# A two-layer hybrid trunk on one core: fewer and larger visits of attention and recurrence between the projections

## The chip, the core and the metric

The kernel runs on one core of a Trainium2 chip. The metric is the device time of one execution in microseconds (us); less is better. Its engines are TensorE (PE: matmuls and, by a matmul with the identity, transposes), VectorE (DVE), ScalarE (ACT), GpSimd (POOL) and SyncE (SP), which issues the weight loads. PE's operands lie in SBUF, its results in eight PSUM banks of 128 x 512 floats. An engine works through its own list of instructions in order, and semaphores make it wait for the others.

## What is computed

Two layers over 256 rows of width 1024, all in float32. Each layer projects the normed rows with one wide matrix, runs a gated linear recurrence (8 heads of 128) and a sliding-window attention with sinks (16 query heads of 64, 4 key heads), merges both with gates, and ends in a gated FFN of width 2816.

```python
h = rmsnorm(x, norm1[l]); proj = h @ w_in[l]
hq, hf, hi, hg, aq, ak, av, ga, gb = split_cols(proj)
q = silu(hq); f = lb + (1 - lb) * sigmoid(hf); kk = 1 - f; v = hi      # per head of 128
o_hg = hgrn2_chunked(q, kk, v, log(max(f, MIN_F)))                     # gated linear recurrence
y_a = (rmsnorm(o_hg, hg_norm[l]) * silu(hg)) @ w_pa[l]
y_b = swa_with_sinks(rope(aq), rope(ak), av, attn_sinks[l]) @ w_pb[l]  # window 128, exp scores
x = x + (sigmoid(ga) * y_a + sigmoid(gb) * y_b) @ w_o[l]
h2 = rmsnorm(x, norm2[l])
x = x + (silu(h2 @ w_gate[l]) * (h2 @ w_up[l])) @ w_down[l]
# after both layers: rmsnorm(x, final_norm)
```

## The kernel before

**Weights.** Every matrix product is made of split operands: `a = ah + al` and `w = wh + wl`, and PE computes `ah wh + ah wl + al wh`. All weights stand in one list, `plan` (lines 154 to 175), in the order in which they are used. SP loads them as blocks of 1 MB (`raw`, three buffers, so loads run ahead). A block is two *units* of 128 x 1024, numbered through the program. For each unit ACT makes `wh` by a cast (`high`, line 221) and DVE makes `wl` by a subtraction (`low`, line 224); five buffers of each (`NW`) let this run about four units ahead (`used`, `ahead`). A unit is used in one of two ways. Form a (line 250) multiplies the activations as weights-in-PE with 512 columns of w: 12 matmuls of 128 x 512, six for each half `t` of the rows. Form b (line 300) computes the transposed product and takes 8 wide (512 columns) and 8 narrow (256 columns) matmuls.

**Order of the projections.** Before, a layer goes akv (keys and values of attention), aq (queries of attention), v (the recurrence's values, eight units), pb (its `f` and `q`, sixteen units in form b, two groups `g` of four heads), gate, gb and yb, ga, ya, wo, then the FFN (`layer`, line 442).

**Sides.** The projections yield after a few matmuls (one step). Two generators run beside them, `attention` (line 577) and `recurrence` (line 783); after each step of the projections the loop `run` (line 435) lets a side take its turn when the number of steps that it yielded has passed. So `YN`, `YD`, `YE`, `YQ` and `GAPS` (lines 31 to 33) are gaps in steps. What a side then puts on PE between two big matmuls is called a *visit* here. `together` lets several generators put their matmuls into one visit; `pe_order` keeps PE's instructions of a visit in the order in which they are written. Otherwise a scheduler sets each engine's order from these calls.

**Attention.** The 16 query heads go in four *attends* n = 0 to 3 of four heads. For each: `qk`, 16 matmuls with 64 contraction rows; then on DVE eight maxima with the mask (`tensor_tensor_reduce`), on ACT eight exponentials in place and one for the sink, on DVE the scaling; `turn(n)`, twelve transposes `pt` of the weights, copied back by ACT; and `values(n)`, 16 matmuls `pv` with 64 output rows. `qp` are the transposes of the queries. One buffer `sp` holds the scores of two attends, so attend n + 2 comes in the visit in which values n are computed: the visits with narrow tiles are qk, qk, pv+qk, pv+qk and pv(2)+pv(3).

**Decays and recurrence.** `decays(g)` (line 601) makes, on ACT, sigmoids of `f` and of `q`, four steps `f = lb + oml f`, and `k = 1 - f`; on DVE `q k` and a maximum. It is issued behind the last attend's exponentials, since sigmoid needs another table of ACT than exp. `chain(g)` (line 613) is the recurrence of four heads: `lb`, `lc` and three `lv` levels of matmuls with 32 or 64 output rows, `lx`, `o` and `ot`, with DVE and ACT work between them. The two chains run one step apart, so visits hold lb(0), then lb(1)+lc(0), lc(1)+lv(0), and so on.

**Opening.** x arrives as 512-column pieces; `Norm.turning` (line 366) turns four 128-column slices on PE, scales them on DVE and splits them on ACT and DVE. `rest(-1)` places the second half's turn behind the first akv matmul. `spin` fills gaps with matmuls `warm` whose result nobody uses.

Of the kernel before, what the change touches and what calls it, by code (L numbers as in the profile page):

```python
# [15 lines left out]
P = 128  # L16
# [26 lines left out]
def trunk(ctx, tc, x, norm1, w_in, lb_logits, hg_norm, attn_sinks, w_pa, w_pb, w_o, norm2,  # L43
# [111 lines left out]
    for l in range(DEPTH):  # L155
        win = w_in[l]
        for c0 in (C_AK, C_AQ, C_AQ + 512, C_HI, C_HI + 512):
            plan += [(win, 0, 4, c0, 512), (win, 4, 4, c0, 512)]
        for g in range(2):
            for col in (C_HF, C_HQ):  # L160
                plan += [(win, 0, KT, col + 512 * g + 256 * b, 256) for b in range(2)]
        for c in range(2):
# [12 lines left out]
        plan.append((w_down[l], groups[-1][0], 2, 0, D))  # L175
# [74 lines left out]
    def form_a(pss, act, skew=False, ks=range(KT), first=True, last=True, late=None):  # L250
# [10 lines left out]
        if late:  # L261
# [61 lines left out]
    def scaled(ps, gain, name):  # L323
        tmp = ztile([P, 4, P], name, "rp")
        V.tensor_tensor(tmp, ps.rearrange("p (k c) -> p k c", k=4),
                        gain.rearrange("p (k o) -> p k o", o=1).to_broadcast([P, 4, P]), ALU.mult)
        return tmp
# [7 lines left out]
    class Norm:  # L335
# [26 lines left out]
        def turn(self, t, c):  # L362
            for _ in self.turning(t, c):
                pass

        def turning(self, t, c):
            ps = psum(f"xp_{self.name}{t}{c}", self.banks[t])
            for j in range(4):
                k = 4 * c + j
                T.transpose(ps[:, j * P:(j + 1) * P], xs[t][:, k * P:(k + 1) * P], ident)  # L370
            sl = slice(t * P, (t + 1) * P)
            ks = slice(4 * c, 4 * c + 4)
            yield
            tmp = scaled(ps, self.gain[:, ks], f"xg_{self.name}{t}{c}")
# [67 lines left out]
    def layer(l, n1):  # L442
# [37 lines left out]
        att = halves(f"att{l}")  # L480
        oT = halves(f"o{l}")
        mT = halves(f"m{l}", "rh")
        fqk = [[btile([P, 4, S], f"{n}{l}{g}", "h") for n in "fqk"] for g in range(2)]
        state = {}
# [19 lines left out]
        def attend(n):  # L504
            g, i0 = n // 2, 2 * (n % 2)
            s = state["sp"][:, n % 2]
            m = sm.tile([P, 4, 2, 2, 2], F32, tag="stat", name=f"stat{l}{n}", bufs=3)
            pss = [[psum(f"qk{l}{n}{t}{u}", "hg" if t else "at") for u in range(2)] for t in range(NT)]
            for t in range(NT):
                W = (t + 1) * P  # L510
                for i in range(2):
                    for u in range(2):
                        pr = slice(u * 64, u * 64 + 64)
                        T.matmul(pss[t][u][:, i * W:(i + 1) * W], qT[g][pr, i0 + i, t * P:(t + 1) * P], kT[pr, g, 0:W],
                                 start=True, stop=True)
            yield
            for t in range(NT):
                W = (t + 1) * P
                for i in range(2):
                    for u in range(2):  # L520
                        V.tensor_tensor_reduce(s[:, 2 * u + i, t * P:t * P + W], pss[t][u][:, i * W:(i + 1) * W],
                                               amask[:, 256 - W:256], op0=ALU.add, op1=ALU.max, scale=1.0,
                                               scalar=-3.0e38, accum_out=m[:, 0, t, u, i:i + 1])
            nsk = nsink.rearrange("p (l g u h) -> p l g u h", l=DEPTH, g=2, u=2)[:, l, g, :, i0:i0 + 2]
            for t in range(NT):
                V.scalar_tensor_tensor(m[:, 1, t], m[:, 0, t], -0.125, nsk, ALU.mult, ALU.min)
                V.tensor_tensor(m[:, 2, t], m[:, 1, t], nsk, ALU.subtract)
            for t in range(NT):
                for u in range(2):
                    for i in range(2):  # L530
                        sv = s[:, 2 * u + i, t * P:t * P + (t + 1) * P]
                        A.activation(sv, sv, AF.Exp, bias=m[:, 1, t, u, i:i + 1], scale=0.125,
                                     accum_out=m[:, 0, t, u, i:i + 1])
            state["exp"] = A.activation(m[:, 2], m[:, 2], AF.Exp).ins
            V.tensor_tensor(m[:, 3], m[:, 0], m[:, 2], ALU.add)
            V.reciprocal(m[:, 3], m[:, 3])
            for t in range(NT):
                for u in range(2):
                    for i in range(2):
                        sv = s[:, 2 * u + i, t * P:t * P + (t + 1) * P]  # L540
                        V.tensor_scalar(sv, sv, m[:, 3, t, u, i:i + 1], None, ALU.mult)

        def turn(n):
            s = state["sp"][:, n % 2]
            for u in range(2):
                ps = psum(f"pt{l}{n}{u}", "at")
                for i in range(2):
                    for t in range(NT):
                        T.transpose(ps[:, i * S + t * P:i * S + t * P + P], s[:, 2 * u + i, t * P:t * P + P], ident)
                A.copy(s[:, 2 * u:2 * u + 2, 0:S], ps.rearrange("p (i c) -> p i c", i=2))  # L550
            ps = psum(f"pt{l}{n}2", "hg")
            for i in range(4):
                T.transpose(ps[:, i * P:(i + 1) * P], s[:, i, 2 * P:3 * P], ident)
            A.copy(s[:, :, S:3 * P], ps.rearrange("p (i c) -> p i c", i=4))

        def values(n, bank):
            g, pT = n // 2, state["sp"][:, n % 2]
            po = psum(f"pv{l}{n}", bank)
            for u in range(2):
                vs = slice(256 + (2 * g + u) * HD, 256 + (2 * g + u + 1) * HD)  # L560
                for i in range(2):
                    o = po[i * 64:i * 64 + 64, u * S:(u + 1) * S]
                    T.matmul(o, akv[0][:, vs], pT[:, 2 * u + i, 0:S], start=True, stop=False)
                    T.matmul(o[:, P:S], akv[1][:, vs], pT[:, 2 * u + i, S:3 * P], start=False, stop=True)
# [12 lines left out]
        def attention():  # L577
            state["sp"] = sm.tile([P, 2, 4, 384], F32, tag="sp", name=f"sp{l}", bufs=1)
            for t in range(NT):
                rope(aq[t], QH, t)  # L580
            yield YQ
            queries(0)
            yield 2
            for n, gaps in enumerate(YN):
                visit = [values(n - 2, "mm")] if n > 1 else []
                together(*visit, attend(n))
                if n == 3:
                    state["last"] = True
                yield gaps[0]
                if n:  # L590
                    turn(n - 1)
                    yield gaps[1]
                if n == 1:
                    queries(1)
                    yield gaps[2]
            turn(3)
            yield YE
            together(values(2, "at"), values(3, "at"))
            yield 5
# [13 lines left out]
        def chain(g):  # L613
# [121 lines left out]
            for i in range(8):  # L735
                h, a = i // 2, i % 2 * P
                T.matmul(ps[0:64, i, :], k[:, h, a:a + 64], q[:, h, a + 64:a + P], start=True, stop=True)
            px = psum(f"lx{l}{g}", tag).rearrange("p (i c) -> p i c", c=P)
# [44 lines left out]
        def recurrence():  # L783
# [4 lines left out]
            yield YD  # L788
            chains = [chain(g) for g in range(2)]
            next(chains[0])  # L790
            yield 1
            while atd[0] is not None:
                yield 1
            for n, gaps in enumerate(GAPS):
                live = [c for g, c in enumerate(chains) if 0 <= n - g < len(GAPS) - 1]
                pe_order[0] = True
                for c in live[::-1]:
                    next(c)
                pe_order[0] = False
                for c, gap in zip(live, gaps):  # L800
                    next(c, None)
                    if n == 0:
                        next(chains[1])
# [13 lines left out]
        for c in range(2):  # L817
            yield from proj(f"v{c}", lambda t, ps: evac_scaled(v[t][:, c * 512:(c + 1) * 512], ps, rs[t]))
# [10 lines left out]
        rec = start(recurrence(), 1)  # L829

# [229 lines left out]
    some = [nx.turning(t, 0) for t in range(NT)]  # L1060
# [5 lines left out]
    go(0)  # L1066
    spin(4)
    prepare()
    high(0, 0)
    go(0, 0)  # L1070
    high(0, 1)
    go(0)
    pinned[0] = False

    def rest(u):
        pinned[0] = True
        if u < 0:
            go(1)
            spin(3)
            go(1, 1)  # L1080
            low(0, 0)
            go(1)
            low(0, 1)
            high(prepare())
            low(1)
            high(prepare())
        elif u == 0:
            some[:] = [nx.turning(t, 1) for t in range(NT)]
# [75 lines left out]
```

## Time and profile before

| what | value |
| --- | --- |
| median of 3 runs | 933.36 us (932.88 to 933.45) |
| the profiled execution, its own time | 933.17 us |
| span of that execution, first to last instruction | 931.4 us |
| mean granted TensorE clock, share of full speed | 0.998 |
| busy PE, DVE, ACT | 923.1, 675.2, 540.8 us |

The span is what the trace covers; 1.77 us of the profiled time lie outside it. A share of busy time is a mean over stages with different limits. In the timelines below, "start" counts from the span's start, the duration of a matmul includes its way through the array, so the distance from one start to the next tells what PE gave to it.

### The profile page before, as it was taken

How to read it: one execution, taken by the hardware profiler on the slowest of the kernel's cores; microseconds unless marked ns; L12 is line 12 of the kernel's file. 1: busy time of each engine (PE TensorE's matmuls, PEld its weight loads, DVE VectorE, ACT ScalarE, POOL GpSimd, SP SyncE). 2: the span in 40 equal slices, each digit the busy share in tenths (PEclk: the TensorE clock that was granted, in tenths of full speed). 3: DMA queues.
4: the chain of work that ended last, by engine and by line, in shares of the span. 5: the costliest groups of instructions: out<-in, count | busy, mean ns of one | idle time of the engine just before them, and what ended most of it. 6: DMA issues, size and time to landing. Idle time of an engine off the chain costs nothing.

```text
span 931.4 us, 14391 instructions
## 1 busy us (share of the span) xinstructions
PE 923.1 (99%) x5726; PEld 781.5 (84%) x5726; DVE 675.2 (72%) x1171; ACT 540.8 (58%) x914; POOL 20.5 (2%) x31
## 2 busy tenths in 40 slices
PE   9999999999999999999999999999999999999997
PEld 7888888888888888888888888888888888888885
DVE  6667789975778766766865677898667777667665
ACT  6566795465456545545555867945554565555553
POOL 2000000001000000000000000000010000000000
PEclk9999999999999999999999999999999999999999
DMA  8735426644546655566465444545445565556531
GB/s 299 259 127 192 136 92 194 205 145 136 181 136 200 198 190 181 186 197 203 163 200 187 136 137 145 173 162 194 151 153 180 165 197 181 181 189 203 194 138 46
DMA packets 111395, 161.40 MB, mean 173 GB/s; under 512 B 2912, under 2 KB 64672, under 8 KB 111328
## 3 DMA queue, kind: packets, MB, share of 16 engines
q1 hardware_dynamic: 110848, 159.42, 52.5%
q8 instruction: 45, 0.74, 0.3%
q10 hardware_dynamic: 320, 0.79, 0.2%
q0 software_dynamic: 160, 0.26, 0.1%
q14 instruction: 22, 0.18, 0.1%
HBM read 159.42 MB, written 1.05 MB: 172 GB/s over the span
## 4 chain that ended last, share of the span: by engine, by line
PE 99%; DVE 0%; ACT 0%; POOL 0%; issue 0%; DVEq 0%; ACTq 0%; POOLq 0%
PE pg L57 13%; PE pu L57 13%; PE acc L57 13%; PE pb L57 10%; PE gate L57 5%; PE gb L57 5%; PE v L57 5%; PE yb L57 5%; PE wo L57 5%; PE ya L57 5%; PE ga L57 5%; PE aq L57 5%; PE akv L57 2%; PE qk L57 1%; PE pv L57 1%; PE o L57 1%
## 5 line engine op out<-in xcount | busy, mean ns | idle before, releaser
L57 DVE TENSOR_TENSOR wl<-raw,wh 128x1024 fp32r<-128x1024 f32 (+1 forms) x301 | 364.3, 1220 | 126.8 <-ACT wh L57 125.4
L57 ACT CAST wh<-raw 128x1024 fp32r<-128x1024 f32 (+1 forms) x301 | 314.5, 1050 | 168.5 <-PE acc L57 46.0
L57 PE MATMUL pu<-xx_n,wh 128*128 128x512 f32 x352 | 92.6, 393 | 0.0
L57 PE MATMUL pg<-xx_n,wh 128*128 128x512 f32 x352 | 92.1, 393 | 0.0
L57 PEld LDWEIGHTS pg<-xx_n,wh 128*128 128x128 f32 x352 | 63.2, 189 | 11.0
L57 PEld LDWEIGHTS pu<-xx_n,wh 128*128 128x128 f32 x352 | 63.1, 189 | 10.9
L57 PE MATMUL acc<-wh,ah 128*128 128x512 f32 x174 | 68.1, 391 | 0.0
L57 PE MATMUL acc<-wh,al 128*128 128x512 f32 x174 | 67.8, 390 | 0.0
L57 PE MATMUL acc<-wl,ah 128*128 128x512 f32 x174 | 67.8, 389 | 0.0
L57 PE MATMUL pb<-xx_n,wh 128*128 128x512 f32 x256 | 66.3, 396 | 0.0
L57 PEld LDWEIGHTS pb<-xx_n,wh 128*128 128x128 f32 x256 | 45.4, 189 | 8.9 <-DVE wl L57 0.7
L57 PEld LDWEIGHTS pg<-xx_n,wl 128*128 128x128 f32 x352 | 48.4, 190 | 4.1 <-ACT xx_n L57 0.6
L57 PEld LDWEIGHTS pu<-xx_n,wl 128*128 128x128 f32 x352 | 48.4, 191 | 3.6
L57 PE MATMUL pg<-xx_n,wl 128*128 128x256 f32 x352 | 50.3, 284 | 0.0
L57 PE MATMUL pu<-xx_n,wl 128*128 128x256 f32 x352 | 49.8, 283 | 0.0
L57 ACT COPY zg<-pg 128x256 f32<-128x256 f32 x44 | 16.4, 372 | 53.1 <-PE pg L57 53.1
L57 PE MATMUL gate<-wh,xx_n 128*128 128x512 f32 x128 | 41.5, 395 | 0.0
L57 ACT ACTIVATE sp<-sp,stat 128x128 f32<-128x128 f32 (+1 forms) x64 | 28.2, 442 | 22.5 <-DVE stat L57 22.5
L57 PE MATMUL gb<-wh,xx_n 128*128 128x512 f32 x128 | 41.2, 393 | 0.0
L57 PE MATMUL ga<-wh,xx_n 128*128 128x512 f32 x128 | 41.0, 394 | 0.0
L57 PE MATMUL v<-wh,xx_n 128*128 128x512 f32 x128 | 40.9, 394 | 0.0
L57 PE MATMUL aq<-wh,xx_n 128*128 128x512 f32 x128 | 40.3, 391 | 0.0
(247 smaller groups left out, 1671.2 us busy)
## 6 DMA issues: line engine op xcount, KB each, us to landing
raw<-in_w_in SPq DMA_DIRECT2D x58, 1024.0 KB, 5.2
raw<-in_w_gate SPq DMA_DIRECT2D x22, 1024.0 KB, 5.1
raw<-in_w_up SPq DMA_DIRECT2D x22, 1024.0 KB, 5.0
raw<-in_w_down SPq DMA_DIRECT2D x22, 1024.0 KB, 5.0
raw<-in_w_pb SPq DMA_DIRECT2D x8, 1024.0 KB, 5.1
raw<-in_w_pa SPq DMA_DIRECT2D x8, 1024.0 KB, 4.9
raw<-in_w_o SPq DMA_DIRECT2D x8, 1024.0 KB, 4.9
raw<-in_w_in SPq DMA_DIRECT2D x3, 512.0 KB, 7.4
```

The source lines that it names most:

```text
L57: ins = call(*args, **kw)
```

## The change

**Recurrence and projections.** pb comes ahead of v, in the weights' list too. The decays follow when the last scores are made (as before, "last" is set after the last qk), so they now stand beside the first v units. The two chains run in step: one visit for lb of both, one for lc of both, and so on; only the second and third level of `lv` are still apart, and lx is separated from its level by a yield.

**Attention.** `attend(g)` now computes the scores of eight heads (two former attends) in one visit. All four values come in one visit at the end. Two more buffers hold scores: `sq` in the place of the recurrence's `pk`, and `sr` in two big tiles of tag "r". Two of the six PSUM tiles of a visit come from the banks of the projections ("mm"). All maxima of both attends stand ahead of their exponentials.

**Opening.** x is turned by two slices at a time in the first half; the first three akv matmuls need only the first slices. `spin` runs with 1 and 1 instead of 4 and 3.

```diff
-YD, YE, YQ = 2, 3, 5
-YN = (8,), (4, 3, 4), (4, 7), (4, 11)
-GAPS = ((8,), (6, 7), (3, 5), (3, 3), (3, 3), (4, 3), (4, 2), (1,))
+YD, YE, YQ = 3, 1, 5
+YN = (6, 5, 4, 2), (6, 5, 7, 3)
+LEV = 3, 3
+GAPS = (6, 6), (6, 6), (5, 5), (4, 4), LEV, (4, 2), (1, 1)
...
-                    order[4:] = [(0, 0, 1, 0), (1, 0, 0, 0), (1, 0, 0, 1), (1, 0, 1, 0), (1, 1, 0, 0), (1, 1, 0, 1), (0, 0, 1, 1),
-                                 (1, 0, 1, 1)]
+                    order = [(0, 0, 0, 0), (0, 1, 0, 0), (0, 0, 1, 0), (0, 0, 0, 1), (0, 1, 0, 1), (1, 0, 0, 0), (1, 0, 1, 0),
+                             (1, 0, 0, 1), (0, 0, 1, 1), (1, 0, 1, 1), (1, 1, 0, 0), (1, 1, 0, 1)]
...
-                    if u == n == 0:
+                    if u == 0 and n == 2:
                         late(-1)
...
-        def attend(n):
...
+        def score(n, u):
+            if n < 2:
+                return state["sp"][:, n, 2 * u:2 * u + 2]
+            return state["sq"][:, 2 * u:2 * u + 2] if n == 2 else state["sr"][u].rearrange(
+                "p a c -> p (a c)")[:, 0:768].rearrange("p (i c) -> p i c", i=2)
+
+        def attend(g):
+            t0 = [psum(f"qk{l}{g}0{u}", "at") for u in range(2)]
+            t1 = [[psum(f"qk{l}{g}1{i0}{u}", "hg" if i0 else "mm") for u in range(2)] for i0 in range(2)]
...
+            for i0, (m, ps) in enumerate(zip(ms, pss)):
+                for t in range(NT)[::-1]:
+                    W = (t + 1) * P
                     for u in range(2):
...
-            for n, gaps in enumerate(YN):
-                visit = [values(n - 2, "mm")] if n > 1 else []
-                together(*visit, attend(n))
-                if n == 3:
+            for g, gaps in enumerate(YN):
+                it = attend(g)
+                together(it)
+                yield gaps[0]
+                next(it)
+                if g == 1:
                     state["last"] = True
...
+            together(*(values(n, ("at", "hg")[n % 2]) for n in range(4)))
             yield YE
-            together(values(2, "at"), values(3, "at"))
-            yield 5
...
             for g in range(2):
                 decays(g)
-            yield YD
-            chains = [chain(g) for g in range(2)]
-            next(chains[0])
-            yield 1
+                yield YD
             while atd[0] is not None:
                 yield 1
-            for n, gaps in enumerate(GAPS):
-                live = [c for g, c in enumerate(chains) if 0 <= n - g < len(GAPS) - 1]
+            chains = [chain(g) for g in range(2)]
+            for c in chains:
+                next(c)
+                yield 3
+            for gaps in GAPS:
                 pe_order[0] = True
-                for c in live[::-1]:
-                    next(c)
+                for _ in range(1 + (gaps is LEV)):
+                    for c in chains:
+                        next(c)
                 pe_order[0] = False
...
     nx = Norm(g1[:, 0], "n1_0")
-    some = [nx.turning(t, 0) for t in range(NT)]
+    some = [nx.turning(t, k, 2) for t in range(NT) for k in (0, 2)]
...
-    go(0)
-    spin(4)
+    go(0, 1)
+    spin(1)
```

How the instructions move. PE at the opening of the program; `xp_n1_000` is the turned x of the first half of the rows, `wh0` and `wl0` the first unit, `akv0_0` the product. Before:

```order
L57 MATMUL xp_n1_000_124<-ident_89,x0_81 128x128 x4
L57 MATMUL warm_96<-ident_89,ones_87 128x128 x4
L57 MATMUL akv0_0_176<-wh0_137,xx_n1_0_119 128x512
L57 MATMUL xp_n1_010_179<-ident_89,x1_82 128x128 x4
L57 MATMUL warm_96<-ident_89,ones_87 128x128 x3
L57 MATMUL akv0_0_176<-wh0_137,xx_n1_0_119 128x512 x3
```

PE at the same place after:

```order
L58 MATMUL xp_n1_000_124<-ident_89,x0_81 128x128 x2
L58 MATMUL xp_n1_002_127<-ident_89,x0_81 128x128 x2
L58 MATMUL warm_96<-ident_89,ones_87 128x128
L58 MATMUL akv0_0_181<-wh0_135,xx_n1_0_119 128x512 x2
L58 MATMUL akv0_0_181<-wl0_136,xx_n1_0_119 128x512
L58 MATMUL xp_n1_010_186<-ident_89,x1_82 128x128 x2
L58 MATMUL xp_n1_012_189<-ident_89,x1_82 128x128 x2
L58 MATMUL warm_96<-ident_89,ones_87 128x128
L58 MATMUL akv0_0_181<-wh0_135,xx_n1_0_119 128x512 x2
```

Three akv matmuls stand ahead of the second half of the rows instead of one, and the warm matmuls went from seven to two.

ACT in layer 0, from the first group's `k` (before) to the first `pk` of the recurrence; `f00` and `k00` are group 0, `f01` and `k01` group 1. Before:

```order
L57 COPY q01_174<-pb0111_1303 128x256
L57 ACTIVATE f00_170<-f00_170,lb_105,oml_106 128x256 x3
L57 ACTIVATE f01_173<-f01_173 128x1024
L57 ACTIVATE k00_172<-f00_170,ones_87 128x1024
L57 ACTIVATE k01_175<-q01_174 128x1024
L57 ACTIVATE f01_173<-f01_173,lb_105,oml_106 128x256 x4
L57 CAST wh40_1361<-raw20_1273 128x1024
L57 ACTIVATE k01_175<-f01_173,ones_87 128x1024
L57 COPY pk00_1372<-q00_171 128x32x32
```

ACT in layer 0 after, the decays from the first group's lb steps to the casts of units 34 and 35, which belong to v's second half. Ahead of these rows stand, behind the second qk visit: the exponentials of two attends with the casts of units 30 and 31 and three copies of pb, the table load and the two sigmoids of group 0.

```order
L58 ACTIVATE f00_175<-f00_175,lb_105,oml_106 128x256 x4
L58 CAST wh32_1174<-raw16_1072 128x1024
L58 ACTIVATE k00_177<-f00_175,ones_87 128x1024
L58 CAST wh33_1192<-raw16_1072 128x1024
L58 ACTIVATE f01_178<-f01_178 128x1024
L58 ACTIVATE k01_180<-q01_179 128x1024
L58 ACTIVATE f01_178<-f01_178,lb_105,oml_106 128x256 x4
L58 COPY sq0_521<-pt020_1211 128x2x256
L58 ACTIVATE k01_180<-f01_178,ones_87 128x1024
L58 COPY sq0_521<-pt021_1217 128x2x256
L58 COPY sq0_521<-pt022_1223 128x2x128 x2
L58 CAST wh34_1236<-raw17_1144 128x1024
```

All decays of both groups stand ahead of the cast of unit 34, with two casts between them; before, the same decays stood ahead of unit 40.

PE in layer 0, at the turns of the last attend (`pt03`). Before, they stand between matmuls of a gate unit, and the next unit's operands follow in their usual order:

```order
L57 MATMUL pt030_1395<-ident_89,sp0_512 128x128 x4
L57 MATMUL pt031_1401<-ident_89,sp0_512 128x128 x4
L57 MATMUL pt032_1407<-ident_89,sp0_512 128x128 x4
L57 MATMUL gate00_0_1329<-wh38_1299,xx_n1_0_119 128x512
L57 MATMUL gate00_0_1329<-wl38_1300,xx_n1_0_119 128x512
```

PE at the same turns after; they stand between units 33 and 34 of v:

```order
L58 MATMUL v10_1_1261<-wh33_1192,xx_n1_0_119 128x512
L58 MATMUL pt030_1296<-ident_89,sr00_165 128x128 x4
L58 MATMUL pt032_1308<-ident_89,sr00_165 128x128 x2
L58 MATMUL pt032_1308<-ident_89,sr01_166 128x128
L58 MATMUL pt031_1302<-ident_89,sr01_166 128x128 x4
L58 MATMUL pt032_1308<-ident_89,sr01_166 128x128
L58 MATMUL v10_0_1260<-wh34_1236,xx_n1_0_119 128x512
L58 MATMUL v10_1_1261<-wh34_1236,xx_n1_0_119 128x512
L58 MATMUL v10_0_1260<-wl34_1237,xx_n1_0_119 128x512
```

Two products with `wh34` stand ahead of the first with `wl34`, and `pt031` came behind most of `pt032`. Between the second qk visit and these turns stand three pb units, 30 matmuls of v, the turns of attend 2 and 42 matmuls of v.

## Rows read from the trace of the kernel before

**Rows 1.** The page, part 1: busy time and share of the span of each engine.

```profile
PE 923.1 (99%) x5726; PEld 781.5 (84%) x5726; DVE 675.2 (72%) x1171; ACT 540.8 (58%) x914; POOL 20.5 (2%) x31
```

**Rows 2.** Timeline (start us, duration, engine, line, operation, out<-in, partitions x elements, count) of PE, a joint visit.

```profile
86.24 1.57 PE L57 MATMUL pv<-sp,akv 128*64 128x256 f32 x16
87.74 1.58 PE L57 MATMUL qk<-kT,qT 64*128 64x128 f32 x16
89.25 0.74 PE L57 MATMUL pb<-xx_n,wl 128*128 128x256 f32 x4
```

**Rows 3.** Timeline of PE, the visit with two heads' groups of values.

```profile
136.57 0.39 PE L57 MATMUL gate<-wh,xx_n 128*128 128x512 f32 x1
136.89 2.87 PE L57 MATMUL pv<-sp,akv 128*64 128x256 f32 x32
139.69 0.50 PE L57 MATMUL gate<-wh,xx_n 128*128 128x512 f32 x1
140.03 0.39 PE L57 MATMUL gate<-wl,xx_n 128*128 128x512 f32 x1
140.26 0.63 PE L57 MATMUL gate<-wh,xx_n 128*128 128x512 f32 x2
```

**Rows 4.** Timeline of PE, part of a unit of form b.

```profile
69.56 1.11 PE L57 MATMUL pb<-xx_n,wl 128*128 128x256 f32 x8
70.50 2.00 PE L57 MATMUL pb<-xx_n,wh 128*128 128x512 f32 x8
```

**Rows 5.** Timeline of PE, twelve turns of scores and the matmul behind them.

```profile
131.36 1.48 PE L57 MATMUL pt<-ident,sp 128*128 128x128 f32 x12
132.59 0.48 PE L57 MATMUL gate<-wh,xx_n 128*128 128x512 f32 x1
```

**Rows 6.** Timeline of DVE, the maxima of the last attend of layer 0.

```profile
109.33 0.28 DVE L57 CUSTOM_DVE_ANT_0 sp<-qk,cf 128x128 f32<-128x128 f32 x1
...
110.17 0.42 DVE L57 CUSTOM_DVE_ANT_0 sp<-qk,cf 128x256 f32<-128x256 f32 x1
...
111.55 0.28 DVE L57 SCALAR_TENSOR_TENSOR stat<-stat,nsink 128x4 f32<-128x4 f32 x2
```

**Rows 7.** Timeline of ACT, its last exponentials and the decays of layer 0.

```profile
111.80 0.40 ACT L57 ACTIVATE sp<-sp,stat 128x128 f32<-128x128 f32 x1 [3.48 <-DVE stat L57]
...
115.43 0.35 ACT L57 COPY f<-pb 128x256 f32<-128x256 f32 x1
...
116.89 1.54 ACT L57 COPY sp<-pt 128x512 f32<-128x512 f32 x3
...
119.40 1.28 ACT L57 ACT_TABLE_LOAD   x1
120.70 1.06 ACT L57 ACTIVATE f<-f 128x1024 f32<-128x1024 f32 x1
...
129.26 1.05 ACT L57 ACTIVATE k<-q 128x1024 f32<-128x1024 f32 x1
130.21 2.07 ACT L57 ACTIVATE f<-f,lb,oml 128x256 f32<-128x256 f32 x4
132.18 1.04 ACT L57 CAST wh<-raw 128x1024 fp32r<-128x1024 f32 x1
133.12 1.16 ACT L57 ACTIVATE k<-f,ones 128x1024 f32<-128x1024 f32 x1
134.17 1.05 ACT L57 COPY pk<-q 128x1024 f32<-128x1024 f32 x1
```

**Rows 8.** Timeline of DVE, a weight unit's low part behind its cast.

```profile
133.25 1.23 DVE L57 TENSOR_TENSOR wl<-raw,wh 128x1024 fp32r<-128x1024 f32 x1 [1.68 <-ACT wh L57]
```

**Rows 9.** Timeline of PE and of ACT, the opening.

```profile
6.33 0.75 PE L57 MATMUL akv<-wh,xx_n 128*128 128x512 f32 x1
...
8.11 0.96 PE L57 MATMUL akv<-wh,xx_n 128*128 128x512 f32 x3
...
7.44 0.62 ACT L57 CAST wh<-raw 128x512 fp32r<-128x512 f32 x1 [1.16 <-DMA raw<-in_w_in]
```

More of the change, by code (lines that the diff above doesn't have):

```diff
@@ L156, in trunk @@
         win = w_in[l]
[L157 removed]
+        for c0 in (C_AK, C_AQ, C_AQ + 512):
             plan += [(win, 0, 4, c0, 512), (win, 4, 4, c0, 512)]
@@ L161, in trunk @@
                 plan += [(win, 0, KT, col + 512 * g + 256 * b, 256) for b in range(2)]
+        for c in range(2):
+            plan += [(win, 0, 4, C_HI + 512 * c, 512), (win, 4, 4, C_HI + 512 * c, 512)]
         for c in range(2):
@@ L362, in turn, with turning @@
         def turn(self, t, c):
-            for _ in self.turning(t, c):
+            for _ in self.turning(t, 4 * c):
                 pass
[L366 to L369, printed above, removed]
+        def turning(self, t, k0, n=4):
+            ps = psum(f"xp_{self.name}{t}{k0}", self.banks[t])
+            for j in range(n):
+                k = k0 + j
                 T.transpose(ps[:, j * P:(j + 1) * P], xs[t][:, k * P:(k + 1) * P], ident)
             sl = slice(t * P, (t + 1) * P)
-            ks = slice(4 * c, 4 * c + 4)
+            ks = slice(k0, k0 + n)
             yield
-            tmp = scaled(ps, self.gain[:, ks], f"xg_{self.name}{t}{c}")
+            tmp = scaled(ps, self.gain[:, ks], f"xg_{self.name}{t}{k0}")
             yield
@@ L480, in layer @@
         att = halves(f"att{l}")
+        state = {"sr": [btile([P, 4, S], f"sr{l}{u}", "r") for u in range(2)]}
         oT = halves(f"o{l}")
@@ new lines, in score @@
+        def score(n, u):
[6 more added lines that the diff above has]
+            t1 = [[psum(f"qk{l}{g}1{i0}{u}", "hg" if i0 else "mm") for u in range(2)] for i0 in range(2)]
+            ms, pss = [], []
+            for i0 in range(2):
+                ms.append(sm.tile([P, 4, 2, 2, 2], F32, tag="stat", name=f"stat{l}{2 * g + i0}", bufs=3))
+                pss.append([[ps[:, i0 * S:i0 * S + S] for ps in t0], t1[i0]])
+                for t in range(NT):
+                    W = (t + 1) * P
+                    for i in range(2):
+                        for u in range(2):
+                            pr = slice(u * 64, u * 64 + 64)
+                            T.matmul(pss[i0][t][u][:, i * W:(i + 1) * W], qT[g][pr, 2 * i0 + i, t * P:(t + 1) * P],
+                                     kT[pr, g, 0:W], start=True, stop=True)
+            yield
+            for i0, (m, ps) in enumerate(zip(ms, pss)):
+                for t in range(NT)[::-1]:
+                    W = (t + 1) * P
+                    for u in range(2):
+                        for i in range(2):
+                            V.tensor_tensor_reduce(score(2 * g + i0, u)[:, i, t * P:t * P + W],
+                                                   ps[t][u][:, i * W:(i + 1) * W], amask[:, 256 - W:256],
+                                                   op0=ALU.add, op1=ALU.max, scale=1.0, scalar=-3.0e38,
+                                                   accum_out=m[:, 0, t, u, i:i + 1])
+            for i0, m in enumerate(ms):
+                n = 2 * g + i0
+                nsk = nsink.rearrange("p (l g u h) -> p l g u h", l=DEPTH, g=2, u=2)[:, l, g, :, 2 * i0:2 * i0 + 2]
+                for t in range(NT):
+                    V.scalar_tensor_tensor(m[:, 1, t], m[:, 0, t], -0.125, nsk, ALU.mult, ALU.min)
+                    V.tensor_tensor(m[:, 2, t], m[:, 1, t], nsk, ALU.subtract)
+                for t in range(NT):
+                    for u in range(2):
+                        for i in range(2):
+                            sv = score(n, u)[:, i, t * P:t * P + (t + 1) * P]
+                            A.activation(sv, sv, AF.Exp, bias=m[:, 1, t, u, i:i + 1], scale=0.125,
+                                         accum_out=m[:, 0, t, u, i:i + 1])
+                state["exp"] = A.activation(m[:, 2], m[:, 2], AF.Exp).ins
+                V.tensor_tensor(m[:, 3], m[:, 0], m[:, 2], ALU.add)
+                V.reciprocal(m[:, 3], m[:, 3])
+                for t in range(NT):
+                    for u in range(2):
+                        for i in range(2):
+                            sv = score(n, u)[:, i, t * P:t * P + (t + 1) * P]
+                            V.tensor_scalar(sv, sv, m[:, 3, t, u, i:i + 1], None, ALU.mult)
+                yield
@@ L548, in turn @@
                     for t in range(NT):
[L549 to L554, printed above, removed]
+                        T.transpose(ps[:, i * S + t * P:i * S + t * P + P], score(n, u)[:, i, t * P:t * P + P], ident)
+                A.copy(score(n, u)[:, :, 0:S], ps.rearrange("p (i c) -> p i c", i=2))
+            ps = psum(f"pt{l}{n}2", "hg").rearrange("p (u i c) -> p u i c", u=2, i=2)
+            for u in range(2):
+                for i in range(2):
+                    T.transpose(ps[:, u, i], score(n, u)[:, i, 2 * P:3 * P], ident)
+            for u in range(2):
+                A.copy(score(n, u)[:, :, S:3 * P], ps[:, u])
         def values(n, bank):
-            g, pT = n // 2, state["sp"][:, n % 2]
+            g = n // 2
             po = psum(f"pv{l}{n}", bank)
@@ L562, in values @@
                     o = po[i * 64:i * 64 + 64, u * S:(u + 1) * S]
-                    T.matmul(o, akv[0][:, vs], pT[:, 2 * u + i, 0:S], start=True, stop=False)
-                    T.matmul(o[:, P:S], akv[1][:, vs], pT[:, 2 * u + i, S:3 * P], start=False, stop=True)
+                    T.matmul(o, akv[0][:, vs], score(n, u)[:, i, 0:S], start=True, stop=False)
+                    T.matmul(o[:, P:S], akv[1][:, vs], score(n, u)[:, i, S:3 * P], start=False, stop=True)
             yield
@@ L829, in layer @@
         rec = start(recurrence(), 1)
+        for c in range(2):
+            yield from proj(f"v{c}", lambda t, ps: evac_scaled(v[t][:, c * 512:(c + 1) * 512], ps, rs[t]))
         def put_gate(c):
@@ L1087, in rest @@
         elif u == 0:
-            some[:] = [nx.turning(t, 1) for t in range(NT)]
+            some[:] = [nx.turning(t, 4) for t in range(NT)]
             go(0, 1, 0, 0, 1, 1, 0, 1)
```

80 lines of the change are left out of this document (21 added, 59 removed).

## The prediction

> **What bounds the kernel now.** I read the page's busy shares first: PE, which is TensorE, is busy in 99% of the span, DVE in 72%, ACT in 58% [rows 1]. So the kernel ends when PE has done its matmuls. A change can take time away only by removing PE time, and can add it only by making PE wait. Next I read PE's timeline around one visit (a group of small matmuls put between the big projections) to see what an interruption costs beyond its own matmuls. Then I read ACT and DVE between the last attend's exponentials and the next weight casts: every weight unit needs a cast on ACT (wh) and a subtraction on DVE (wl), and attention and decays share these engines. Busy share hides this; ACT's 58% is a mean, and in that stretch its rows follow each other without a gap.
>
> **The visits: a gain.** The wide matmul's cadence is 0.23 us (140.03 to 140.26). Before a visit with narrow tiles the last wide one takes 0.32 (136.57 to 136.89), behind it the first one takes 0.34 (139.69 to 140.03): 0.20 more for one interruption. Inside, two groups of values take 2.80 (136.89 to 139.69), one group alone 1.50 (86.24 to 87.74); 2 x 1.50 - 2.80 = 0.20 is paid once per visit whatever its length [rows 2, 3]. A lone visit so costs 0.40. Where pv is followed by qk [rows 2] the tile shape changes once more, and I add the same 0.20. Before, attention has three lone visits and two joint ones per layer: 3 x 0.40 + 2 x 0.60 = 2.40. After, it has two of qk and one of pv, each of one shape: 1.20. Gain 1.2 per layer. That qk behaves as pv is an estimate; the trace has no visit with two attends of qk. The recurrence has one narrow visit fewer and fewer changes of shape inside: one times 0.40 at most, taken as 0.35. Big matmuls and transposes stay the same in number outside the opening. Sum for both layers: 2 x (1.2 + 0.35) = 3.1; from 2.2 (the inner 0.20 not saved) to 3.5.
>
> **The opening: a small gain.** PE's first akv matmul is at 6.33, then one waits for the second weight slice, whose cast runs from 7.44 to 8.06, and eleven akv matmuls of unit 0 are left at 8.11 [rows 9]. With x turned in halves, three akv matmuls instead of one can run ahead of that slice; two fewer stand behind it, 2 x 0.23 = 0.46. The cast at 7.44 waits for a DMA that the change leaves alone, so nothing before 8.1 counts. The price is five warm matmuls fewer, so PE idles in gaps that were filled. In these rows one wide akv matmul takes 0.75 at 6.33 and three take 0.96 at 8.11: the granted clock goes from 1.2 to 2.4 GHz between them, after PE was busy without a break. If gaps delay that, nine matmuls at double cadence lose 9 x 0.23 = 2.1. I take -0.4, with bounds -0.5 and +1.7.
>
> **The decays' place: a loss.** This decides the sign. Let T be the end of the second qk visit, and let unit 34 be the third unit of v's second half. I count what ACT must do, in its new order, before it can cast wh34.
>
> First, when it starts. Both attends' maxima stand ahead of the exponentials on DVE. For one attend they take 0.84 (109.33 to 110.17) + 1.38 (110.17 to 111.55) = 2.22, for two 4.44, and the first exponential follows 0.25 later (111.55 to 111.80) [rows 6, 7]. Ahead of the maxima DVE has wl29, which waits for wh29, which waits for a copy of the projection that ends about 3.0 before T (the visit's length: 2.80 and entry): copy 0.26, cast 1.04, subtraction 1.23 [rows 7, 8], so the maxima start at about T - 0.4 and the exponentials at T + 4.3. The earliest possible is T + 3.3, when the first attend's scores alone hold them up.
>
> From there ACT's list, all by starts of [rows 7]: the exponentials of one attend 3.63 (111.80 to 115.43); two copies and wh30 1.46 (115.43 to 116.89); the other attend 3.63; a copy 0.26; wh31 1.04; the table load with its gap 1.30 (119.40 to 120.70); two sigmoids 1.90 (0.95 each, 129.26 to 130.21); four lb steps 1.97 (130.21 to 132.18); wh32 0.94 (132.18 to 133.12); k 1.05 (133.12 to 134.17); wh33 0.94; the second group's two sigmoids 1.90, lb steps 1.97 and k 1.05; the copies of three score turns 1.54 (the row of 116.89); wh34 1.04. Sum 25.6. So wh34 is ready at T + 29.9, and wl34, 1.23 later, at T + 31.1.
>
> Now PE, if it never waits: three units of form b, each 0.94 (eight narrow, 69.56 to 70.50) + 8 x 0.23 = 2.78, together 8.3; 72 matmuls of v at 0.227, 16.3; two visits of twelve turns, 1.23 (131.36 to 132.59) + 0.08 at the exit, 2.6 [rows 4, 5]. It wants wh34 at T + 27.3, and wl34, with two products put ahead of it, at T + 27.75. 31.1 - 27.75 = 3.35: PE stands idle for about 3.3 us, part of it already in the last turns, whose PSUM buffer waits for a copy that lies behind the decays on ACT. With the early start it is 2.4. The other bound, 3.8, takes half a microsecond of hand-over between engines into account. Layer 1 has the same order, so it is twice this: +6.6, from 4.8 to 7.6. Before, the same decays ran behind one attend's exponentials and with gate units due later; PE has no gap there.
>
> The Trainium skill, "ScalarE: Activation LUTs", section "What ACT_TABLE_LOAD costs", says that a switch of tables costs a drain on top of the load, about 2.66 us in all. The row shows 1.30 from the load's start to the next activation's [rows 7], and the trace decides. By the page's figure the estimate would be 1.4 later per layer, 2.7 in all.
>
> **Small terms.** DVE's work between the joint lb visit and the joint lc visit doubles, since both groups are now worked on at once; counted by hand it ends within 0.3 of when PE wants it, which I take as +0.1 per layer, from 0 to 0.3. The reordered projections cost PE nothing: same weights, same shapes, and the loads are fetched in the new order too.
>
> **Sum.** Profiled time 933.17, of which 931.4 is the span. -3.1 - 0.4 + 6.6 + 0.2 = +3.3, so 936.5; the median of the runs is 0.19 above the profiled one, so I say 936.6. Its own range, by the bounds without a late clock: -4.0 + 4.8 = +0.8 to -2.4 + 7.6 + 0.6 = +5.8, or 934.2 to 939.2.
>
> **Rivals.**
> *ACT's list hides (faster).* Place: between T and unit 34. If the list takes 22.3 or less instead of 25.6, or the exponentials and casts meet PE's need in some way I don't see, there is no stall and only the gains stand: 933.36 - 3.5 = 929.9. For it: before has no stall with the same decays. Against it: ACT executes in order, the list has no waiting in it, and two attends lie ahead of the decays now, not one. Chance 0.14.
> *Half a stall (no change).* Exponentials at T + 3.3 or shorter gaps, 1 to 2 per layer lost: 931.9 to 933.9. It decides where DVE finishes wl29. Chance 0.14.
> *A late or lost clock (slower still).* The opening's gaps delay the full clock: +2.1 on the forecast, 938.7. Or the clock falls in the stall of unit 34: at the opening the half-rate stretch reaches from the start beyond 6.33 [rows 9], and half of some 5 us, twice, adds 5: 941.6. The Trainium skill, "TensorE: Matmul & The Clock Gate", section "Part 1: The HAM clock gate (the "warmup" mystery)", says that an idle PE returns to half rate; before has no such gap, so no row here shows it. Chance 0.10 together.
> *The visits don't get cheaper.* If the inner 0.20 belongs to each attend, the joint visit saves half as much: 937.7. The 2.80 against twice 1.50 speaks against it. Chance 0.04, and its time lies in the forecast's range.
>
> **How the numbers follow.** Forecast with a stall of about 3.3 per layer: 0.58 (with the visits' rival 0.62). About 0.2%, 1.9 us, is what a measurement of this kernel tells from no change: 931.5 to 935.2. Faster takes the first rival and a little of the second, 0.16; the same takes the rest of the second and the forecast's lower end, 0.22; slower 0.62. The range leaves out the hidden list and the lost clock: 931.5 to 939.4.
>
> **What would show it.** Right: PE idle for some 3 us just before v's unit 34 in each layer, released by ACT's wh and DVE's wl; ACT without a gap from the first exponentials to that cast; five narrow visits per layer in attention become three with 0.40 each; unit 0 of akv ends 0.4 earlier. Wrong: no PE gap there, or ACT idle in that stretch, or the full clock coming later than at 8.11.

## The result, and the profile after

The changed kernel takes 937.32 us (median of 5 runs, 937.02 to 938.14), the kernel before in the same session 933.45. The ratio is 1.0046 (95% interval 1.0034 to 1.0057): slower by 0.46%, where 936.6 was forecast. The profiled execution took 937.61, its span is 935.8, 4.4 longer than before.

The page's part 1 for the changed kernel, and the first line of its part 4, the chain of work that ended last:

```profile
PE 922.8 (99%) x5716; PEld 781.6 (84%) x5716; DVE 674.5 (72%) x1175; ACT 541.7 (58%) x924; POOL 19.3 (2%) x31
...
PE 92%; ACT 6%; DVE 2%; issue 0%; POOL 0%; DVEq 0%; ACTq 0%; POOLq 0%
```

The busy shares hardly differ from [rows 1]: PE's busy time even fell by 0.3 us, and its longer span is idle time. The chain shows where: 6% of it now runs through ACT and 2% through DVE; before, PE had 99% of it and these two 0%. PE's waits (what it waited for, us in total, times, longest) name the units:

```profile
PE v L58 <- DVE wl L58: 2.6, 4, 0.8
PE warm L58 <- POOL ident L58: 1.6, 1, 1.6
PE v L58 <- ACT wh L58: 1.4, 2, 0.7
PE pt L58 <- ACT sq L58: 0.6, 2, 0.3
```

The wait for `ident` is the program's start, and it is the only one that the kernel before has:

```profile
PE warm L57 <- POOL ident L57: 1.6, 1, 1.6
```

The others are new: v's weights and the copies of the turns. PE's timeline in layer 0, from v's unit 32 to its unit 34:

```profile
110.12 0.70 PE L58 MATMUL v<-wh,xx_n 128*128 128x512 f32 x2
111.58 0.50 PE L58 MATMUL v<-wl,xx_n 128*128 128x512 f32 x1 [0.77 <-DVE wl L58]
111.92 0.62 PE L58 MATMUL v<-wh,xx_n 128*128 128x512 f32 x2
...
116.93 0.92 PE L58 MATMUL pt<-ident,sr 128*128 128x128 f32 x7
118.18 0.77 PE L58 MATMUL pt<-ident,sr 128*128 128x128 f32 x5 [0.32 <-ACT sq L58]
119.66 0.73 PE L58 MATMUL v<-wh,xx_n 128*128 128x512 f32 x2 [0.71 <-ACT wh L58]
120.92 0.50 PE L58 MATMUL v<-wl,xx_n 128*128 128x512 f32 x1 [0.53 <-DVE wl L58]
121.26 0.39 PE L58 MATMUL v<-wh,xx_n 128*128 128x512 f32 x1
```

Read it by starts. A modelled matmul lasts longer than its share of PE, so the bracketed waits understate the loss. From 110.12 to 111.58 two matmuls take 1.46 where 0.46 is usual: 1.0. The last turns take 2.73 (116.93 to 119.66) where the same twelve took 1.23 [rows 5]: 1.5. From 119.66 to 120.92 two matmuls take 1.26 instead of some 0.54: 0.7. With 0.1 more behind each of the two gaps in v it is 3.4 us in this layer, and the same in layer 1. ACT's timeline beside it:

```profile
94.01 0.40 ACT L58 ACTIVATE sq<-sq,stat 128x128 f32<-128x128 f32 x1 [5.81 <-DVE stat L58]
...
97.64 0.62 ACT L58 COPY q<-pb 128x256 f32<-128x256 f32 x2
98.16 1.05 ACT L58 CAST wh<-raw 128x1024 fp32r<-128x1024 f32 x1
99.11 0.40 ACT L58 ACTIVATE sr<-sr,stat 128x128 f32<-128x128 f32 x1
...
102.99 1.05 ACT L58 CAST wh<-raw 128x1024 fp32r<-128x1024 f32 x1
104.06 1.28 ACT L58 ACT_TABLE_LOAD   x1
...
109.24 1.03 ACT L58 CAST wh<-raw 128x1024 fp32r<-128x1024 f32 x1
...
117.56 1.10 ACT L58 COPY sq<-pt 128x512 f32<-128x512 f32 x3
118.55 2.00 ACT L58 CAST wh<-raw 128x1024 fp32r<-128x1024 f32 x2
```

From the first exponential at 94.01 to the casts at 118.55 no row starts behind a gap. The cast at 109.24 is wh32, the first of the two at 118.55 is wh34.

The visits, then the akv matmuls of the opening and its end, PE:

```profile
86.78 2.89 PE L58 MATMUL qk<-kT,qT 64*128 64x128 f32 x32
89.60 0.73 PE L58 MATMUL pb<-xx_n,wh 128*128 128x512 f32 x2
...
124.77 2.87 PE L58 MATMUL pv<-sp,akv 128*64 128x256 f32 x32
127.42 1.52 PE L58 MATMUL pv<-sq,akv 128*64 128x256 f32 x16
128.72 1.52 PE L58 MATMUL pv<-sr,akv 128*64 128x256 f32 x16
130.18 0.50 PE L58 MATMUL v<-wh,xx_n 128*128 128x512 f32 x1
...
8.21 1.63 PE L58 MATMUL akv<-wh,xx_n 128*128 128x512 f32 x3
9.64 0.63 PE L58 MATMUL akv<-wl,xx_n 128*128 128x512 f32 x1
...
20.41 0.39 PE L58 MATMUL aq<-wh,xx_n 128*128 128x512 f32 x1
```

Two attends of scores take 2.82 in one visit (86.78 to 89.60); before, a group of one attend took 1.51 (87.74 to 89.25, [rows 2]), so 0.20 is saved. Four groups of values take 5.41 (124.77 to 130.18); two took 2.80 [rows 3], so again 0.20. In the opening the three akv matmuls at 8.21 take 1.43 from start to start (to 9.64), 0.48 each, still twice the cadence of 0.23; before, the three at 8.11 [rows 9] took 0.80 (to 8.91). The first aq matmul, the end of the opening, starts at 20.41; in the kernel before it starts here:

```profile
19.91 0.39 PE L57 MATMUL aq<-wh,xx_n 128*128 128x512 f32 x1
```

### The profile page after: what moved, and what is told of

The parts are those of the page before. It is cut to its first block, busy times and chain, and to the rows that moved or that the text cites. A ratio compares the mean times of both kernels' runs of the same rounds, so it can differ in the third digit from the quotient of the medians.

```text
span 935.8 us, 14401 instructions
## 1 busy us (share of the span) xinstructions
PE 922.8 (99%) x5716; PEld 781.6 (84%) x5716; DVE 674.5 (72%) x1175; ACT 541.7 (58%) x924; POOL 19.3 (2%) x31
## 3 DMA queue, kind: packets, MB, share of 16 engines
HBM read 159.42 MB, written 1.05 MB: 171 GB/s over the span
## 4 chain that ended last, share of the span: by engine, by line
PE 92%; ACT 6%; DVE 2%; issue 0%; POOL 0%; DVEq 0%; ACTq 0%; POOLq 0%
PE pg L58 13%; PE pu L58 13%; PE acc L58 13%; PE pb L58 8%; PE yb L58 5%; PE gb L58 5%; PE wo L58 5%; PE gate L58 5%; PE ga L58 5%; PE ya L58 5%; PE aq L58 5%; PE akv L58 3%; ACT f L58 1%; ACT wh L58 1%; PE v L58 1%; PE pv L58 1%
## 5 line engine op out<-in xcount | busy, mean ns | idle before, releaser
L58 PEld LDWEIGHTS acc<-wh,al 128*128 128x128 f32 x174 | 32.7, 188 | 6.9
```

The lines of the kernel that those rows point to most:

```text
L58: ins = call(*args, **kw)
```

## The experiments

Times are medians of 5 or 11 runs; the kernel before ran beside them at 933.0 to 933.2, beside the changed kernel at 933.45.

| run | time | ratio to before (95%) |
| --- | --- | --- |
| the changed kernel | 937.32 | 1.0046 (1.0034 to 1.0057) |
| decays apart | 939.2 | 1.0067 (1.0054 to 1.0080) |
| maxima split | 932.48 | 0.9994 (0.9985 to 1.0003) |
| ACT longer | 940.67 | 1.0079 (1.0066 to 1.0092) |
| warm matmuls kept | 938.39 | 1.0049 (1.0036 to 1.0061) |
| apart and split | 931.33 | 0.9980 (0.9971 to 0.9989) |
| the same, lc later | 931.66 | 0.9982 (0.9974 to 0.9991) |
| opening of before | 937.43 | 1.0049 (1.0035 to 1.0062) |
| opening alone | 932.79 | 0.9999 (0.9990 to 1.0008) |
| six steps apart | 931.11 | 0.9980 (0.9971 to 0.9989) |
| six steps, pv later | 930.23 | 0.9963 (0.9949 to 0.9976) |

**Maxima split.** The second attend's maxima come behind the first one's statistics:

```diff
                                                    accum_out=m[:, 0, t, u, i:i + 1])
-            for i0, m in enumerate(ms):
                 n = 2 * g + i0
```

> The changed kernel, with the maxima of a visit's second attend behind the first attend's statistics, so that the first exponentials start after 2.2 us of maxima instead of 4.4. Nothing else of ACT's list is taken away. Theory (the list starts too late and is too long): the whole list moves 2.2 us earlier, unit 32 no longer waits, unit 34 waits for about 1.2 us: 937.3 - 2 x 2.2 = 932.9. Rival (the start of the list does not matter, since ACT waits for PE's pb results or for DVE further on): no change, 937.3.

932.48: 4.8 less than the changed kernel, where 4.4 was expected. PE's timeline of this run in layer 0 shows the turns whole again and what is left at unit 34:

```profile
115.78 1.47 PE L58 MATMUL pt<-ident,sr 128*128 128x128 f32 x12
117.42 0.50 PE L58 MATMUL v<-wh,xx_n 128*128 128x512 f32 x1 [0.17 <-ACT wh L58]
118.68 0.50 PE L58 MATMUL v<-wl,xx_n 128*128 128x512 f32 x1 [0.76 <-DVE wl L58]
```

About 1.4 is left per layer: 0.4 ahead of the first matmul with wh34, 0.9 between it and the first with wl34, 0.1 behind. Unit 32 has no wait. From the first aq matmul to the span's end, which leaves the opening's scatter out, the run takes 911.2 and the changed kernel 915.4, 4.3 less. So when ACT's list starts does set PE's wait.

**ACT longer.**

```diff
             A.activation(k, f, AF.Identity, bias=ones[:, 0:1], scale=-1.0)
+            if g == 0:
+                A.activation(k, f, AF.Identity, bias=ones[:, 0:1], scale=-1.0)
```

> The changed kernel, with the step that makes k of group 0 done twice on ACT, 1.05 us more in the list ahead of wh34; the output is the same. Theory (ACT's list is the bound there): PE waits 1.05 us longer per layer, 937.3 + 2.1 = 939.4. Rival (another wait ends last, so ACT has slack): 937.3.

940.67, which is 3.35 more, not 2.1 and not 0. The rows tell the two parts from each other. From the start of the second qk visit to the first matmul with wl34 PE takes 35.18 in layer 0 (85.72 to 120.90), where the changed kernel takes 34.14 (86.78 to 120.92): 1.04 more, and 1.04 in layer 1 too. That is the longer list, so ACT's list is the bound. What comes on top is the clock. Windows of this run behind the wait of layer 0 (window, its length, busy time of PE, PEld, DVE, ACT and POOL, PEclk, then DMA):

```profile
121.00:123.00 2.00, 2.00 (x5) 1.61 (x6) 1.32 (x2) 2.00 (x4) 0.00 (x0) 0.50 0.00 0
```

The granted clock is 0.50 there, 1.2 GHz, where the profiled execution of the changed kernel has 1.00. Five wide matmuls fit in 2 us instead of nine. From that matmul with wl34 to the pv visit PE takes 5.03 and 5.44 in the two layers of this run and 3.85 in both layers of the changed kernel.

**Decays apart.**

```diff
             for g in range(2):
                 decays(g)
-                yield YD
+                yield 3 if g else 10
```

> The changed kernel, with the decays of group 1 started ten steps of the projections behind those of group 0 instead of three. On ACT its sigmoids, lb steps and k (5.9 us) then stand behind the cast of unit 36 instead of ahead of that of unit 34. Theory (PE waits because ACT's list ahead of wh34 is too long): wh34 comes 5.9 us earlier and the wait at unit 34 and in the turns ahead of it (2.4 us per layer) is gone; the wait at unit 32 (1.0 us per layer), whose cast stands behind group 0's decays, stays. 937.3 - 2 x 2.4 = 932.6. Rival (PE waits for the copies that free the turns' PSUM buffers, or for a weight load): the place of the decays changes nothing, 937.3.

939.2: slower, and neither theory had that. PE's waits in this run:

```profile
PE lc L58 <- DVE p L58: 4.7, 2, 2.4
...
PE v L58 <- DVE wl L58: 1.5, 2, 0.8
PE pv L58 <- ACT sr L58: 0.4, 2, 0.2
```

The wait at unit 34 and in the turns is gone as the theory said, unit 32's stayed as it said, but 2.4 us per layer came up at the joint lc visit:

```profile
156.30 0.89 PE L58 MATMUL lc<-p,k 128*32 128x48 f32 x64
159.54 1.51 PE L58 MATMUL lc<-p,k 128*32 128x48 f32 x64 [2.35 <-DVE p L58]
160.97 0.80 PE L58 MATMUL gb<-wh,xx_n 128*128 128x512 f32 x1
161.57 0.63 PE L58 MATMUL gb<-wl,xx_n 128*128 128x512 f32 x1
```

DVE writes group 1's `p` at about the same hour as in the changed kernel (its last piece starts at 158.97 here, at 159.07 there). PE is earlier and so waits. Group 1's decays, its products, lb and p are one chain of ACT and DVE work. In the changed kernel the wait at unit 34 had covered it. Behind the new wait the matmuls take 0.60 and 0.43 from start to start: the clock fell here too (granted clock 0.50 in the window 160 to 162).

**Both edits, and lc later.** The second run of this pair differs from the first by `GAPS = (8, 7), (6, 6), ...` instead of `(6, 6), (6, 6), ...`.

> Both edits on the changed kernel: maxima of the two attends apart, and group 1's decays ten steps behind group 0's. Simple theory (only the cast of units 32 and 34 was late): no wait is left, 932.5 less the 1.25 us per layer that PE still waited with the maxima apart, 930.0. Theory of the chain (decays of group 1, its first products on DVE, lb, its second products, lc: one chain of ACT and DVE work, which the later decays put off, while PE comes earlier): PE waits at the joint lc visit for DVE's p, 1.2 to 3.4 us per layer, 932.4 to 936.8, more where the clock falls behind the wait.

> The run with both edits (maxima apart, group 1's decays later), and the joint lc visit put 90 big matmuls behind lb instead of 72, 4.1 us later; the later visits keep their distances. Theory of the chain: DVE has its p ready by then, PE has no wait in units 32 and 34 nor at lc, 930.0. Rival (DVE as a whole is behind, since the weights' subtractions stand in its list too): a wait stays at lc or comes at a later visit, 932 or more.

931.33 and 931.66. With both edits the waits at units 32 and 34 are gone, and lc's is about 0.26 (its visit takes 1.77 instead of 1.51), so the chain theory's 1.2 to 3.4 was too much, and the simple theory was nearer. With lc later that 0.26 is gone too and no later visit waits, yet the median is no lower and misses that theory's 930.0. Both have a wait that neither text named:

```profile
PE pv L58 <- ACT sr L58: 1.0, 2, 0.5
```

By starts it is 0.58 per layer: pv waits for the copies of the last turns, only 18 matmuls ahead of it.

**Six steps, and pv later.** First 6 steps between the groups' decays instead of 10, then `YN = ..., (6, 5, 7, 5)` instead of `(6, 5, 7, 3)` on top.

> The run with both edits (maxima apart, group 1's decays later), but with six steps between the two groups' decays instead of ten: group 1's sigmoids and lb steps then stand on ACT behind the cast of unit 34 and ahead of that of unit 35, and no longer ahead of the copies of the last turns, for which pv waited 0.58 us per layer in that run. Theory (each wait is where ACT's list puts the decays): no wait at units 32 and 34, at pv or at lc, 931.3 - 2 x 0.58 - 2 x 0.26 = 929.7. Rival (the copies of the last turns are late anyway, since the casts of units 36 and 37 stand ahead of them): pv waits as before, 931.3 or 930.8.

931.11: pv waited as before. The rival was right: the copies of the last turns stand behind the casts of units 36 and 37, here the pair at 117.95, and the decays' place does not matter for them. ACT in this run:

```profile
117.95 2.00 ACT L58 CAST wh<-raw 128x1024 fp32r<-128x1024 f32 x2
119.84 1.61 ACT L58 COPY sr<-pt 128x512 f32<-128x512 f32 x4
```

> The run with six steps between the decays of the two groups, and the visit of all values two steps later, 30 matmuls behind the last turns instead of 18 (2.7 us); lb, lc and the rest move along. Theory (pv waits for ACT's copies of the last turns, which stand behind two casts): the 0.58 us per layer at pv is gone and lc keeps its wait of about 0.27: 931.1 - 1.2 = 929.9. Rival (the wait moves on to lb or lc, as it did before): 931.1.

930.23, 0.9963 of the kernel before. The wait did not move on, and lc's, which was expected to stay, is gone as well (the visit takes 1.51, 158.19 to 159.70). From the first aq matmul on the run takes 908.3 and the one with six steps 910.0. PE's only wait of this kernel, and its chain:

```profile
PE warm L58 <- POOL ident L58: 1.6, 1, 1.6
...
PE 99%; DVE 0%; ACT 0%; issue 0%; POOL 0%; DVEq 0%; ACTq 0%; POOLq 0%
```

This kernel beats both.

**The opening.** Three runs: the changed kernel with `spin(4)` and `spin(3)`, the changed kernel with the whole opening of before, and the kernel before with only the new opening.

> The changed kernel, with four and three warm matmuls in the opening, as in the kernel before, instead of one and one. Theory (the thinner work of PE at the opening lets the full clock come later, near 10 us instead of near 7): the matmuls behind 8.2 us run at full clock, the first aq matmul starts at 19.6 to 19.9 us instead of 20.41, time 936.6. Rival (the clock rises when it does whatever fills the gaps): the first aq matmul at 20.4 to 20.9, time 937.3 to 937.8.

> The changed kernel with the opening of the kernel before (turns of four slices, one akv matmul ahead of the second slice, four and three warm matmuls). Theory A (the new opening costs time, since its full clock comes later): first aq matmul at 19.9 us, 936.8. Theory B (the new opening gains 0.4 and the hour at which the clock rises is not tied to it): first aq at 19.9 to 20.4, 937.3 to 937.8.

> The kernel before with the opening of the changed kernel and nothing else. Theory A: first aq matmul at 20.4 us, 933.5 to 933.9. Theory B: first aq at 19.3 to 20.4 from run to run, 932.6 to 933.6, as often faster as slower.

938.39, 937.43 and 932.79 (932.22 to 935.14). The first aq matmul of these runs and of the run with six steps, which has the new opening as it is (warm kept, opening of before, opening alone, six steps):

```profile
20.11 0.39 PE L58 MATMUL aq<-wh,xx_n 128*128 128x512 f32 x1
...
19.67 0.39 PE L58 MATMUL aq<-wh,xx_n 128*128 128x512 f32 x1
...
19.38 0.39 PE L57 MATMUL aq<-wh,xx_n 128*128 128x512 f32 x1
...
18.96 0.39 PE L58 MATMUL aq<-wh,xx_n 128*128 128x512 f32 x1
```

The nine profiled executions with the new opening run from 18.96 to 20.50, the two with the old one have 19.67 and 19.91. The hour at which the full clock comes moves from one execution to the next: with the same opening it came before the matmul at 7.44 in one run and not before 10 us in another. (The granted-clock column reads 1.00 through the whole opening in every run, so the rate there is read from the starts alone.) Theory B is nearer. With warm matmuls kept aq starts at 20.11, between what the theory and the rival expected, so that run decides nothing on the opening. Whether the new opening is worth 0.4 on the mean can't be settled at this spread; alone, it makes no difference that can be measured.

In the run with warm matmuls kept the time is above the changed kernel's for another reason. Windows of it behind the wait at unit 34 of layer 0, then the same windows of the changed kernel:

```profile
119.00:121.00 2.00, 1.09 (x3) 0.66 (x4) 1.64 (x2) 2.00 (x4) 0.00 (x0) 0.91 0.00 0
121.00:123.00 2.00, 2.00 (x6) 1.52 (x6) 1.32 (x2) 2.00 (x3) 0.00 (x0) 0.50 0.12 15
123.00:125.00 2.00, 2.00 (x8) 1.64 (x7) 1.77 (x2) 2.00 (x6) 0.00 (x0) 0.74 0.92 306
```

```profile
119.00:121.00 2.00, 0.82 (x3) 0.38 (x3) 1.36 (x2) 2.00 (x3) 0.00 (x0) 1.00 0.00 0
121.00:123.00 2.00, 2.00 (x9) 1.66 (x10) 1.31 (x2) 2.00 (x4) 0.00 (x0) 1.00 0.00 0
123.00:125.00 2.00, 2.00 (x11) 1.39 (x11) 2.00 (x2) 2.00 (x6) 0.00 (x0) 1.00 0.86 224
```

The waits are the same, yet the clock fell in the one and not in the other. The five executions of the run part in the same way: three with a mean granted clock of 0.996 took 938.39 to 938.74, two with 0.998 took 936.07 and 936.89, near the theory's 936.6; two are too few to show that warm matmuls gain something.

## Why the prediction was right, and where it was off

**The decays' place: right, in kind and size.** T, the end of the second qk visit, is 89.60 in layer 0. The list was to start at T + 4.3 = 93.9, and did at 94.01. wh34 was to be ready at T + 29.9 = 119.5; PE's first matmul with it starts at 119.66. wl34 was to come at T + 31.1 = 120.7; its first matmul starts at 120.92. The wait was worked out as 3.35 per layer and is 3.4. The run in which PE waits nowhere behind the start, six steps with pv later, agrees: from the qk visit to the pv visit it takes 34.54 (86.88 to 124.14, less 2.72 for the twelve matmuls by which its pv comes later), the changed kernel 37.99, 3.45 more. It fell on three places, not one: 1.0 of it already at unit 32, whose cast stands behind group 0's decays. The prediction named the turns but not unit 32; the sum is unaffected, since the list's end sets it. Maxima split and ACT longer show by experiment that start and length of the list are what counts: 2.2 us earlier took 2.0 off, 1.05 us more added 1.04.

**The visits: right.** The span grew by 4.4: 0.5 by the opening (19.91 to 20.41), the rest 3.9, 1.95 per layer. With 3.4 of waits and 0.1 at lc, the visits gave back 3.5 - 1.95 = 1.55 per layer, the 1.2 + 0.35 of the forecast. That is a remainder, but it can be read directly too, from the last matmul ahead of a visit to the second behind it, less the usual share of two such matmuls. Attention's narrow visits in layer 0 take 12.85 before (1.71, 1.71, 3.21, 3.22, 3.00) and 11.65 after (3.02, 3.03, 5.60), 1.20 less; the recurrence's take 18.66 and 18.31, the wait at lc included. And that run without waits takes 908.3 from the first aq matmul on where the kernel before takes 911.5, 3.2 less; 3.1 was forecast. That qk behaves as pv was an estimate and held: 0.20 each.

**The opening: the step that failed.** -0.4 was taken, the profiled execution has +0.5. This is most of what the forecast missed: the other terms add up to +3.7, and the rows give 3.9. One of the prediction's signs of being wrong came with it, the full clock later than at 8.11. The mechanism of the matmuls is there: where the full clock came early, the first aq matmul starts at 18.96 to 19.38. In ACT longer and opening alone it starts at 19.34 and 19.38, ahead of the 19.91 before, although the rate rose a little later there (four turns at 7.08 and 7.07 took 0.59 and 0.62 from start to start, at 6.92 before 0.44). The step that failed is that the clock's hour was taken as fixed but for the gaps that the change makes. It scatters over some 3 us or more among the nine executions with this opening: four turns at 6.84 took 0.44 in the run with six steps, and a wide akv matmul at 10.06 still took 0.43 in pv later. That is worth 1.5 us at the first aq. The bound of +1.7 held it. Whether the gaps put the hour off on the mean stays open: both profiled executions with the old opening had the full rate by 6.92.

**The small term at lc: right in size, wrong in meaning.** The lc visit takes 1.63 in layer 0 where 1.51 is its length without a wait, so 0.12 against the 0.1 forecast. But it was put down as independent of the wait at unit 34. Decays apart shows that it is not: remove the one and 2.4 appears at the other. It depends on how the wait is removed: in maxima split, where the whole list comes earlier, unit 34 loses 2.0 and lc has no wait (1.50). So the rival of the hidden list, 929.9, could not have been had by moving only the second group's decays.

**The drain of the table load.** The next activation starts 1.30 behind the load's start (104.06; the sigmoid's row starts at 105.36), as in [rows 7]. The trace decided rightly.

**The lost clock.** As a rival it had 0.10 with the late clock. It is no other outcome but part of this one: the clock falls behind the wait in some executions, and the changed kernel's five runs scatter over 1.1 us, before's over 0.7; the slowest, 938.14, has a mean granted clock of 0.996, the others 0.997 and 0.998. The loss in the run with warm matmuls kept is about 1.6 in one layer (from the first matmul with wl34 to pv 5.43, 120.64 to 126.07, against 3.85), and in ACT longer 1.2 and 1.6, less than the 2.5 per layer that the rival had. The Trainium skill, "TensorE: Matmul & The Clock Gate", section "Part 1: The HAM clock gate (the "warmup" mystery)", has an idle PE return to half rate, and says that the moment at which the rate rises at a start varies between runs. The rows here agree with both, 0.50 behind the waits and a first aq matmul from 18.96 to 20.50, and show besides that the fall too comes in one execution and not in another with the same waits, with matmuls running between them.

## What to carry to other kernels

When PE is the bound, list what the helper engine must do, in its new order, between two points that PE can't move, and compare the sum with PE's own work between them; shares of busy time (58% for ACT) say nothing on it. Merging visits saved what the rows said, but it also gathered the helpers' work into one stretch, and that cost twice the gain; spreading the maxima and the decays again and putting pv later gave 930.23 from the same visits. After removing a wait, look for the next consumer on the same chain before counting the gain: decays apart removed 2.4 us per layer and lost all of it 40 us later.

## What the runs showed of the hardware that was not expected

- A PE wait of some 2 to 3 us in pieces, with matmuls between, can be followed by some 3 us at 1.2 GHz (granted clock 0.91, 0.50 and 0.74 in the three windows of the run with warm matmuls kept), in some executions and not in others with the same waits. So a stall can cost more than its length: in the profiled execution of ACT longer 1.2 and 1.6 us came on top of the wait in the two layers.
- The hour of the full clock at the program's start differs between executions of one opening: first aq matmul at 18.96 to 20.50. A gain of 0.4 us there can't be read from one profile.
